# A deeper ring of early weight loads, and the context loaded behind the modulation weights

## The chip, the cores and the metric

One core of a Trainium2 chip runs the whole program. The metric is the time of one execution in microseconds, as the device measures it. The kernel before was run three times: 2746.86 us in the median, from 2741.91 to 2751.96.

## What is computed

Sequence x has 512 tokens, a context 256 tokens, the model width is 2048. Both are normalised, scaled and shifted by a modulation that is worked out from a conditioning vector, and projected to the queries, keys, values and gates of four kinds of attention (branches A to D). The attention outputs go through a gated output projection and are added to x. Two further layers of the same sort follow. The part at the start, which the change touches, reads in short:

```python
mod = silu(c) @ w_ada + b_ada            # shift, scale, gate: 3 x 2048
h   = rms_norm(x,   norm_g) * (1 + scale_x) + shift_x
hc  = rms_norm(ctx, norm_g) * (1 + scale_c) + shift_c
y   = h  @ w_in                          # all projections of the sequence
yc  = hc @ w_in[:, context columns]      # keys and values of the context
...
x   = x + gate * (attention(y, yc) @ w_out)
```

Every product is in float32. The kernel splits each operand into a rounded part (fp32r) and the remainder, and forms three products of 128x512 from the two pairs.

## The kernel before

**Order.** The program's steps are Python generators. At build time a list scheduler runs them against its own table of costs and a clock, and fixes one order of instructions for each engine: PE (TensorE), ACT (ScalarE), DVE (VectorE), POOL (GpSimd) and SP (SyncE, which issues the loads). A step asks for a slot of a pool of buffers, waits for an event, or names an engine and a cost. Each engine runs its row of instructions in order; a change of a slot or a mark therefore moves rows on every engine.

**Weight stream.** `stream()` (L499) takes the list of weight units, each 128x512 float32 (256 KB), two of them a pair. `loads()` issues the pairs on SP, each into the slots that `ring(i)` (L515) names: a pair takes one slot of `wr`, one of `pt`, or two of `P`, in turn, for the first 160 units. There are two slots of 1024 columns in `wr` and in `pt`, five of 768 in `P` and three of 768 in `p`; `pt`, `P` and `p` are pools of the attention and stand empty at the start. `hi()` writes the rounded half of a unit on ACT (L554), `lo()` the remainder on POOL or DVE (L564), and `main()` runs the products in the order of the units. A slot comes free when both units of its pair have been used. After issuing pair i//2, `loads()` sets a mark of that number; other loads wait for marks.

**First units.** There are 128 modulation units (`ada_units`, L630): shift and scale, four blocks each of 512 columns. Their weights go to TensorE as they are, in groups of four units (L667). When a block is whole, `finish()` copies the sums, transposes them by a product with `sel` (L641) and writes `modv` (L647, L656). Among them stand 24 units of six projections: a quarter of the depth (512 of the 2048 rows) of each of six tiles, in four rounds. The shift and scale of quarter b allow the hx blocks of that quarter, and the six units of quarter b follow in the stream. The six of the last quarter end it. The text calls the stretches with the products of these rounds the first to the last quarter. Their accumulators are two tiles named px, one pc, two S and one O. After them come the tiles of keys and values, which take x and the context together.

**Inputs.** `inputs()` (L705) loads x and the context four blocks of 128 rows at a time (`xt`, L717), each load behind a mark; `XMARK` and `CMARK` give the first mark and the distance. It squares every block on ACT (L729), adds on DVE or POOL (L734, L744), and forms the reciprocal norm (L391, L358 to L365, L376, L380, L383). `make_h()` (L758) makes the blocks hx of x and hc of the context from it: a product with the norm (L772, DVE or POOL), scale and shift on ACT (L786), and the split into two parts (L288 on ACT, L291 on DVE or POOL). In the kernel before the context's marks are 40, 46, 52 and 58.

**Behind it.** `gate()` (L673) loads the 64 blocks of gate weights (`gw`, L269) and sums them on DVE (L693, L695); it starts when the last hc block is made. `tables()` builds the tables of relative positions with L1646.

Of the kernel before, what the change touches and what calls it, by code (L numbers as in the profile page):

```python
# [16 lines left out]
DRAM = bass.MemoryType.DRAM  # L17

KT = 16
EARLY = 160  # L20
LAG = (12, 4)
WAYS = 3
EARLY_OUT = ["px", "px", "pc"]
D_ORDER = "r0 q0 h0 q1 g0 h1 g1 r1 g2 q2 h2 g3 q3 - h3"
XMARK = (4, 0.4)
CMARK = (40, 6)
EPS = 1e-6
NEG = -1e30
LOG2 = math.log(2)
# [12 lines left out]
def f32(ap):  # L42
    return ap.bitcast(F32)
# [136 lines left out]
def D(n=0, x2=False, k=1, ptr=0):  # L180
    return ("DVE", k * (0.075 + n * (0.52e-3 if x2 else 1.04e-3) + 0.053 * ptr))
# [7 lines left out]
def A(n=0, ptr=0, acc=0, k=1):  # L189
    return ("ACT", k * (0.1 + n * 0.833e-3 + 0.093 * (ptr + acc)))  # L190


def G(n=0, k=1, bias=0.0):

    return ("POOL", k * (0.1 + n * 2.2e-3), bias)
# [13 lines left out]
class Net:  # L209
# [294 lines left out]
    def stream(self):  # L504

        ready = [Ev() for _ in self.units]
        raws = [Ev() for _ in range((len(self.units) + 1) // 2)]
        left = [min(2, len(self.units) - i) for i in range(0, len(self.units), 2)]
        nc = self.nc

        def whole(i):

            return len(self.units[i]) > 2

        def ring(i):  # L515

            return (["wr"], ["pt"], ["P", "P"], ["wr"], ["pt"], ["P", "P"])[i // 2 % 6] if i < EARLY else ["wr"]

        def wring(i):
            return ("w", "act")[i % 2] if i < EARLY else "w"  # L520

        def loads():
            for i in range(0, len(self.units), 2):
                n = min(2, len(self.units) - i)
                tags = ring(i)
                raw = yield from self.alloc(tags[0], name="wr")
                raw = [raw[:, :512], raw[:, 512:]] if len(tags) == 1 else [raw[:, :512]]
                if len(tags) > 1:
                    raw.append((yield from self.alloc(tags[1], name="wr"))[:, :512])
                src = [self.units[i + j][0] for j in range(n)]  # L530
                if n == 2 and len(tags) == 1 and src[1].offset == src[0].offset + 512:
                    both = bass.AP(tensor=raw[0].tensor, offset=raw[0].offset, ap=[raw[0].ap[0], [1, 1024]])
                    x = src[0]
                    src = [bass.AP(tensor=x.tensor, offset=x.offset, ap=[x.ap[0], [1, 1024]])]
                    dst = [both]
                else:
                    dst = raw
                for x, y in zip(dst, src):
                    yield ("SP", 0.06)
                    nc.sync.dma_start(x, y)  # L540
                self.dma_free = max(self.dma_free, self.s.now) + 1.46
                self.s.set_at(raws[i // 2], self.dma_free + 1.9, raw)
                self.s.set(self.marks.setdefault(i // 2, Ev()))

        def hi():
            for i in range(len(self.units)):
                yield raws[i // 2]
                r = raws[i // 2].val[i % 2]
                if whole(i):
                    self.s.set(ready[i], r)  # L550
                    continue
                w = yield from self.alloc(wring(i), (2, 512), F32R, "w")
                yield A(512)
                nc.scalar.activation(w[:, 0], r, AF.Copy)  # L554
                self.spawn(lo(i, w, r), 1)

        def used(i):
            left[i // 2] -= 1
            if left[i // 2] == 0:
                self.free(*ring(i))  # L560

        def lo(i, w, r):
            e = yield [D(512), G(512, bias=WSLACK)]
            (nc.gpsimd if e == "POOL" else nc.vector).tensor_tensor(w[:, 1], r, f32(w[:, 0]), op=OP.subtract)  # L564
            used(i)
            self.s.set(ready[i], w)

        def main():
            for i, (_, fn, *_) in enumerate(self.units):
                if fn is None:  # L570
                    continue
                if whole(i):
                    for j in range(i, i + 4):
                        yield ready[j]
                    yield from fn([ready[j].val for j in range(i, i + 4)])
                    for j in range(i, i + 4):
                        used(j)
                    continue
                yield ready[i]
                w = ready[i].val  # L580
                yield from fn(w[:, 0], w[:, 1])
                self.free(wring(i))
        self.spawn(loads(), 0)
        self.spawn(hi(), 1)
        self.spawn(main(), 9)
# [633 lines left out]
    def block1(self):  # L1219
# [55 lines left out]
        def ctx():  # L1275
            rc = (yield from self.alloc("b", name="rc"))[:, :256]
            cs, cfin = self.inputs(a["cT"], 256, rc, 4, *CMARK)
            self.make_h(cs, cfin, 256, rc, 1, mods, hc, 4)
# [1098 lines left out]
```

## Time and profile before

| what | value |
|---|---|
| median of three runs | 2746.86 us (2741.91 to 2751.96) |
| profiled execution, its own time | 2743.26 us |
| its span in the profile | 2741.2 us |
| TensorE busy | 2659.6 us, 97% of the span |
| VectorE, ScalarE, GpSimd busy | 1471.3, 1164.1, 1098.7 us |
| DMA | 315.98 MB, 115 GB/s in the mean |
| instructions | 36539 |

The span is the stretch that the profile shows; the execution's own time lies 2.1 us above it. Busy times add up what each engine did. TensorE's products are pipelined, so one row of 0.39 us stands in a dense row of products every 0.23 us. "PEclk" is the clock that was granted to TensorE as a share of its full speed. A note in brackets after an instruction of a timeline gives the idle time before it and what ended that.

### The profile page before, as it was taken

How to read it: one execution, taken by the hardware profiler on the slowest of the kernel's cores; microseconds unless marked ns; L12 is line 12 of the kernel's file. 1: busy time of each engine (PE TensorE's matmuls, PEld its weight loads, DVE VectorE, ACT ScalarE, POOL GpSimd, SP SyncE). 2: the span in 40 equal slices, each digit the busy share in tenths (PEclk: the TensorE clock that was granted, in tenths of full speed). 3: DMA queues.
4: the chain of work that ended last, by engine and by line, in shares of the span. 5: the costliest groups of instructions: out<-in, count | busy, mean ns of one | idle time of the engine just before them, and what ended most of it. 6: DMA issues, size and time to landing. Idle time of an engine off the chain costs nothing.

```text
span 2741.2 us, 36539 instructions
## 1 busy us (share of the span) xinstructions
PE 2659.6 (97%) x13324; PEld 2189.9 (80%) x13324; DVE 1471.3 (54%) x3242; ACT 1164.1 (42%) x2361; POOL 1098.7 (40%) x886
## 2 busy tenths in 40 slices
PE   7889999999999999999999999999999999999999
PEld 3468888888888887788888878777888888888887
DVE  2457753336552656522368576765215877777500
ACT  3444433333332455433442445454334555555421
POOL 1351333334333333344445544445444333344544
PEclk8989999999999999999999999999999999999999
DMA  9845542222221213244222322224442222222443
GB/s 348 301 166 182 171 144 75 76 72 74 70 71 61 70 65 112 88 144 144 85 85 93 108 85 87 90 78 142 148 140 91 94 87 99 90 80 85 143 139 126
DMA packets 121960, 315.98 MB, mean 115 GB/s; under 512 B 13874, under 2 KB 23986, under 8 KB 121780
## 3 DMA queue, kind: packets, MB, share of 16 engines
q1 hardware_dynamic: 121780, 313.65, 34.4%
q8 instruction: 104, 1.70, 0.3%
q14 instruction: 76, 0.62, 0.1%
HBM read 293.02 MB, written 32.11 MB: 119 GB/s over the span
## 4 chain that ended last, share of the span: by engine, by line
PE 80%; DVE 13%; DMA 2%; ACT 2%; issue 1%; POOL 1%; SPq 0%; DVEq 0%; POOLq 0%; ACTq 0%
PE px L491 20%; PE px L492 20%; PE px L493 20%; PE T L398 4%; PE S L1113 2%; PE pc L496 1%; PE pc L498 1%; PE pc L497 1%; DVE P L1803 1%; DVE P L1815 1%; PE T L412 1%; DVE P L314 1%; PE O L1088 1%; PE O L1089 1%; DVE sm L1820 1%
## 5 line engine op out<-in xcount | busy, mean ns | idle before, releaser
L564 POOL TENSOR_TENSOR w<-wr,w 128x512 fp32r<-128x512 f32 x696 | 919.5, 1322 | 1423.1 <-ACT w L554 1419.0
L554 ACT ACTIVATE w<-wr 128x512 fp32r<-128x512 f32 x736 | 463.2, 630 | 948.4 <-PE px L493 616.0
L491 PE MATMUL px<-u,w 128*128 128x512 f32 x1248 | 498.5, 399 | 0.0
L492 PE MATMUL px<-u,w 128*128 128x512 f32 x1248 | 488.8, 392 | 0.0
L493 PE MATMUL px<-u,w 128*128 128x512 f32 x1248 | 488.4, 391 | 0.0
L491 PE MATMUL px<-hx,w 128*128 128x512 f32 x816 | 331.9, 407 | 9.4 <-ACT w L554 6.3
L492 PE MATMUL px<-hx,w 128*128 128x512 f32 x816 | 323.2, 396 | 2.2 <-POOL hx L291 2.2
L493 PE MATMUL px<-hx,w 128*128 128x512 f32 x816 | 322.3, 395 | 1.7 <-POOL w L564 1.7
L491 PE MATMUL px<-o,w 128*128 128x512 f32 x752 | 295.0, 392 | 3.3 <-ACT o L288 3.3
L492 PE MATMUL px<-o,w 128*128 128x512 f32 x752 | 294.3, 391 | 0.5 <-DVE o L291 0.5
L493 PE MATMUL px<-o,w 128*128 128x512 f32 x752 | 294.0, 391 | 0.0
L493 PEld LDWEIGHTS px<-u,w 128*128 128x128 f32 x1248 | 234.8, 188 | 51.3
L491 PEld LDWEIGHTS px<-u,w 128*128 128x128 f32 x1248 | 236.1, 189 | 40.7 <-issue 0.3
L492 PEld LDWEIGHTS px<-u,w 128*128 128x128 f32 x1248 | 235.7, 189 | 39.6
L291 DVE TENSOR_TENSOR pt<-T,pt 128x512 fp32r<-128x512 f32 (+2 forms) x208 | 127.0, 616 | 111.7 <-ACT pt L288 110.3
L493 PEld LDWEIGHTS px<-hx,w 128*128 128x128 f32 x816 | 154.9, 190 | 38.7 <-POOL w L564 3.3
L491 PEld LDWEIGHTS px<-hx,w 128*128 128x128 f32 x816 | 155.7, 191 | 32.9 <-ACT w L554 9.0
L492 PEld LDWEIGHTS px<-hx,w 128*128 128x128 f32 x816 | 155.7, 191 | 19.8 <-POOL hx L291 2.7
L491 PEld LDWEIGHTS px<-o,w 128*128 128x128 f32 x752 | 142.2, 189 | 33.4 <-ACT o L288 4.0
L492 PEld LDWEIGHTS px<-o,w 128*128 128x128 f32 x752 | 142.1, 189 | 30.5 <-DVE o L291 1.1
L493 PEld LDWEIGHTS px<-o,w 128*128 128x128 f32 x752 | 142.0, 189 | 29.3
L1598 DVE TENSOR_TENSOR xr<-px,xr 128x512 f32<-128x512 f32 x32 | 22.1, 692 | 251.0 <-PE px L493 248.1
(343 smaller groups left out, 4365.2 us busy)
## 6 DMA issues: line engine op xcount, KB each, us to landing
wr<-w SPq DMA_DIRECT2D x237, 512.0 KB, 3.5
wr<-wout SPq DMA_DIRECT2D x89, 512.0 KB, 4.2
wr<-wada SPq DMA_DIRECT2D x37, 512.0 KB, 6.8
gw<-wada SPq DMA_DIRECT2D x64, 256.0 KB, 5.3
wr<-w SPq DMA_DIRECT2D x58, 256.0 KB, 4.0
wr<-wada SPq DMA_DIRECT2D x54, 256.0 KB, 6.0
x<-xr SPq DMA_DIRECT2D x32, 256.0 KB, 4.3
xr<-x SPq DMA_DIRECT2D x32, 256.0 KB, 4.5
```

Source lines behind the costliest of these rows:

```text
L291: eng.tensor_tensor(lo, src, f32(hi), op=OP.subtract)
L314: self.nc.vector.tensor_scalar(dst, src, col, None, op0=OP.mult)
L398: self.nc.tensor.transpose(p[:, j * 128:(j + 1) * 128], x, self.ident)
L412: nc.tensor.matmul(p[:, j * gq:(j + 1) * gq], sq[:, j * 128:(j + 1) * 128], self.ones[:, 0:1] if gq == 1 else self.halves, start=True, sto ...
L491: mm(px, hi[:, s], x[0], **kw)
L492: mm(px, hi[:, s], x[1], start=False, stop=False)
L493: mm(px, lo[:, s], x[0], **ke)
L496: mm(pc, lo[:, s], c[0], **kw)
L497: mm(pc, hi[:, s], c[0], start=False, stop=False)
L554: nc.scalar.activation(w[:, 0], r, AF.Copy)
L564: (nc.gpsimd if e == "POOL" else nc.vector).tensor_tensor(w[:, 1], r, f32(w[:, 0]), op=OP.subtract)
L1113: self.nc.tensor.matmul(o, l, r, start=i == 0, stop=i == len(ops) - 1)
```

## The change

The ring of the early units takes turns over seven pairs instead of three: the two slots of one more pair come from the pool `p`, and the turn is wr, pt, P P, p p, wr, pt, P P, so that 14 units instead of 12 can be ahead, up to unit 140. From there to unit 160 the old turn holds. The context's marks become 66, 69, 72 and 75. Lines after L517 of the changed file are numbered two higher.

```diff
-EARLY = 160
+EARLY = 140, 160
...
-CMARK = (40, 6)
+CMARK = (66, 3)
...
         def ring(i):
 
-            return (["wr"], ["pt"], ["P", "P"], ["wr"], ["pt"], ["P", "P"])[i // 2 % 6] if i < EARLY else ["wr"]
+            if i < EARLY[0]:
+                return (["wr"], ["pt"], ["P", "P"], ["p", "p"], ["wr"], ["pt"], ["P", "P"])[i // 2 % 7]
+            return (["wr"], ["pt"], ["P", "P"])[i // 2 % 3] if i < EARLY[1] else ["wr"]
 
         def wring(i):
-            return ("w", "act")[i % 2] if i < EARLY else "w"
+            return ("w", "act")[i % 2] if i < EARLY[1] else "w"
```

TensorE's rows are the same in number and kind, and the orders of all engines differ only in about the first 300 us. Three places follow.

ACT at the start of the third quarter, before; `b` are blocks being made, `hx` the rounded half of a block, L729 squares of the context, and L554 the rounded half of the first weights of the quarter:

```order
L786 ACTIVATE b_825<-b_825,modv 128x512
L288 ACTIVATE hx_835<-b_825 128x512
L786 ACTIVATE b_826<-b_826,modv 128x512
L288 ACTIVATE hx_837<-b_826 128x512
L786 ACTIVATE b_827<-b_827,modv 128x512
L288 ACTIVATE hx_839<-b_827 128x512
L786 ACTIVATE b_828<-b_828,modv 128x512
L288 ACTIVATE hx_853<-b_828 128x512
L729 ACTIVATE b_802<-xt_790 128x256
L729 ACTIVATE b_804<-xt_790 128x256
L729 ACTIVATE b_816<-xt_790 128x256
L554 ACTIVATE w_847<-wr_833 128x512
```

The same place of the changed kernel:

```order
L788 ACTIVATE b_795<-b_795,modv 128x512
L288 ACTIVATE hx_805<-b_795 128x512
L788 ACTIVATE b_796<-b_796,modv 128x512
L288 ACTIVATE hx_807<-b_796 128x512
L556 ACTIVATE w_776<-wr_773 128x512
L788 ACTIVATE b_797<-b_797,modv 128x512
L288 ACTIVATE hx_809<-b_797 128x512
L788 ACTIVATE b_798<-b_798,modv 128x512
L288 ACTIVATE hx_822<-b_798 128x512
L556 ACTIVATE w_848<-wr_817 128x512
```

The squares of the context are gone from here, and the half of the weights (L556 now) stands behind two hx blocks instead of four.

SP where the context's last two loads stood before (`xt<-cT`):

```order
L540 DMA wr_730<-w 128x512
L540 DMA wr_733<-wada 128x1024
L717 DMA xt_728<-cT 128x1024
L540 DMA wr_755<-wada 128x1024
L540 DMA wr_757<-wada 128x512
L540 DMA wr_758<-wada 128x512
L540 DMA wr_780<-wada 128x1024
L540 DMA wr_786<-wada 128x1024
L540 DMA wr_791<-wada 128x512
L540 DMA wr_792<-wada 128x512
L717 DMA xt_790<-cT 128x1024
```

SP where they stand in the changed kernel, `wada` being modulation weights and `w` the weights of projections:

```order
L542 DMA wr_937<-wada 128x512
L542 DMA wr_954<-wada 128x512
L542 DMA wr_960<-wada 128x512
L542 DMA wr_960<-w 128x512
L719 DMA xt_963<-cT 128x1024
L542 DMA wr_985<-w 128x512 x2
L542 DMA wr_995<-w 128x512
L542 DMA wr_996<-w 128x512
L542 DMA wr_999<-w 128x512 x2
L719 DMA xt_1003<-cT 128x1024
L542 DMA wr_1034<-w 128x1024
```

Both have moved behind the last modulation weights, among the loads of the last quarter's weights.

DVE at the start of the last quarter, before; `rx` and `rc` are the norms of x and of the context, `modv` the scale and shift:

```order
L305 COPY b_1125<-T_988 128x512
L564 TENSOR_TENSOR w_1129<-wr_1087,w_1129 128x512
L564 TENSOR_TENSOR w_1153<-wr_1095,w_1153 128x512
L647 TENSOR_SCALAR modv<-T_1137,vec 128x2 x4
L772 TENSOR_TENSOR b_1172<-xt_148,rx 128x512
L772 TENSOR_TENSOR b_1173<-xt_148,rx 128x512
L772 TENSOR_TENSOR b_1174<-xt_150,rx 128x512
L772 TENSOR_TENSOR b_1175<-xt_150,rx 128x512
L772 TENSOR_TENSOR b_1179<-xt_790,rc_92 128x256
L291 TENSOR_TENSOR hx_1186<-b_1173,hx_1186 128x512
L291 TENSOR_TENSOR hx_1190<-b_1174,hx_1190 128x512
L291 TENSOR_TENSOR hx_1195<-b_1175,hx_1195 128x512
```

And in the changed kernel:

```order
L305 COPY b_1033<-T_909 128x512
L736 TENSOR_TENSOR b_846<-b_846,b_1028 128x256
L566 TENSOR_TENSOR w_1038<-wr_995,w_1038 128x512
L649 TENSOR_SCALAR modv<-T_1047,vec 128x2 x4
L566 TENSOR_TENSOR w_1073<-wr_999,w_1073 128x512
L774 TENSOR_TENSOR b_1084<-xt_132,rx 128x512
L774 TENSOR_TENSOR b_1085<-xt_132,rx 128x512
L774 TENSOR_TENSOR b_1086<-xt_134,rx 128x512
L774 TENSOR_TENSOR b_1087<-xt_134,rx 128x512
L291 TENSOR_TENSOR hx_1094<-b_1084,hx_1094 128x512
L291 TENSOR_TENSOR hx_1098<-b_1085,hx_1098 128x512
L291 TENSOR_TENSOR hx_1103<-b_1086,hx_1103 128x512
```

The product of a context block has left the place behind the four of x, and the last sums of the context's squares (L736) and two remainders of weights (L566) stand ahead.

## Rows read from the trace of the kernel before

**Rows 1.** Stretches: length, busy us (PE, PEld, DVE, ACT, POOL), clock, DMA share, GB/s.

```profile
0.00:73.00 73.00, 54.36 (x237) 23.89 (x238) 20.39 (x64) 22.63 (x37) 12.13 (x13) 0.86 0.96 349
73.00:107.00 34.00, 30.12 (x156) 17.53 (x154) 10.13 (x25) 11.83 (x23) 9.66 (x8) 0.95 0.93 323
107.00:149.50 42.50, 37.40 (x172) 20.38 (x170) 23.54 (x56) 26.38 (x54) 24.74 (x23) 0.88 0.76 267
149.50:186.00 36.50, 27.42 (x96) 19.47 (x97) 28.65 (x43) 18.91 (x35) 20.13 (x17) 0.77 0.30 97
186.00:250.00 64.00, 63.74 (x378) 55.48 (x377) 38.95 (x70) 20.05 (x39) 12.53 (x9) 1.00 0.63 205
```

**Rows 2.** TensorE's timeline, second quarter: start us, us, engine, line, operation, tiles, count, [idle].

```profile
73.02 0.95 PE L641 MATMUL T<-sel,b 128*128 128x2 f32 x8
...
83.11 0.80 PE L493 MATMUL px<-hx,w 128*128 128x512 f32 x1 [0.67 <-POOL w L564]
...
86.95 1.07 PE L667 MATMUL T<-wr,cst 128*32 128x512 f32 x8
...
106.84 0.95 PE L641 MATMUL T<-sel,b 128*128 128x2 f32 x8
```

**Rows 3.** ScalarE's timeline, start of the second quarter.

```profile
75.24 0.81 ACT L786 ACTIVATE b<-b,modv 128x512 f32<-128x512 f32 x1 [3.71 <-DVE b L772]
...
77.99 0.80 ACT L786 ACTIVATE b<-b,modv 128x512 f32<-128x512 f32 x1
...
80.73 0.40 ACT L729 ACTIVATE b<-xt 128x256 f32<-128x256 f32 x1
81.03 0.61 ACT L554 ACTIVATE w<-wr 128x512 fp32r<-128x512 f32 x1
```

**Rows 4.** TensorE's timeline, third quarter.

```profile
118.82 0.80 PE L493 MATMUL px<-hx,w 128*128 128x512 f32 x1 [0.40 <-POOL w L564]
...
125.09 1.94 PE L667 MATMUL T<-wr,cst 128*32 128x512 f32 x8
...
147.62 0.95 PE L641 MATMUL T<-sel,b 128*128 128x2 f32 x8
```

**Rows 5.** ScalarE's timeline, start of the third quarter.

```profile
110.14 0.82 ACT L786 ACTIVATE b<-b,modv 128x512 f32<-128x512 f32 x1 [1.94 <-DVE b L772]
...
116.54 0.61 ACT L554 ACTIVATE w<-wr 128x512 fp32r<-128x512 f32 x1
```

**Rows 6.** SyncE's DMA queue, third quarter: start us, us that the issues took.

```profile
115.77 12.10 SPq L540 DMA_DIRECT2D wr<-wada  x3
```

**Rows 7.** Stretches inside the third quarter, columns as in rows 1.

```profile
116.00:128.00 12.00, 9.92 (x29) 5.57 (x30) 6.21 (x16) 3.02 (x8) 4.90 (x4) 0.57 0.42 161
128.00:140.00 12.00, 11.94 (x69) 7.37 (x67) 6.96 (x19) 10.33 (x23) 10.34 (x11) 1.00 0.93 305
140.00:150.00 10.00, 8.65 (x48) 5.32 (x40) 4.71 (x9) 6.11 (x12) 10.00 (x9) 1.00 0.75 248
```

**Rows 8.** TensorE's timeline, last quarter and start of the first context tile.

```profile
155.51 0.79 PE L492 MATMUL px<-hx,w 128*128 128x512 f32 x1 [2.22 <-POOL hx L291]
...
175.28 0.80 PE L491 MATMUL S<-hx,w 128*128 128x512 f32 x1 [2.45 <-ACT th L928]
...
178.33 0.79 PE L491 MATMUL S<-hx,w 128*128 128x512 f32 x1 [1.41 <-DVE th L930]
...
185.27 0.39 PE L491 MATMUL px<-hx,w 128*128 128x512 f32 x1
...
185.95 0.28 PE L496 MATMUL pc<-hc,w 128*128 128x256 f32 x1
```

**Rows 9.** The gate's tile gw: ns min/median/max, first and last start.

```profile
L695 DVE SCALAR_TENSOR_TENSOR gacc<-gw,csil,gacc x60: 732/745/1784, 178.2 to 379.9; 128x512 f32<-128x512 f32 x60
```

**Rows 10.** ScalarE's groups for hc, 100 to 260 us: busy us, mean ns, idle.

```profile
L786 ACT ACTIVATE b<-b,modv 128x256 f32<-128x256 f32 x16 | 9.4, 587 | 0.5 <-DVE b L772 0.5
L288 ACT ACTIVATE hc<-b 128x256 fp32r<-128x256 f32 x16 | 6.6, 415 | 0.4
```

## The prediction

> **What bounds the kernel now.** I read the busy times by stretch first, then TensorE's timeline, then ScalarE's, and the DMA queue's last. The stretches of [rows 1] show where anything can be won: from 186 us on TensorE is busy 63.74 of 64 us at a granted clock of 1.00, while before that it is busy 54.36 of 73, 30.12 of 34, 37.40 of 42.5 and 27.42 of 36.5 us, at 0.86, 0.95, 0.88 and 0.77. Most of what the change moves lies ahead of 186 us. The first 73 us move 349 GB/s at a DMA share of 0.96, so transfers bound them. The third quarter does not look like that: its share is 0.76, and inside it [rows 7] show 161 GB/s at 0.42 between 116 and 128 us, at a clock of 0.57. Here a chain of engines holds the end. TensorE's first remainder product of the quarter runs at 118.82 and waits for GpSimd's remainder of the weights [rows 4]; that waits for ScalarE's rounded half, which starts at 116.54 [rows 5], behind four blocks of hx and squares of the context. Meanwhile three issues of modulation weights take SyncE 12.10 us from 115.77 on [rows 6]: its slots come free only when TensorE has read them. The last quarter starts with a similar chain, and its products wait again at 175.28 and 178.33 [rows 8].
>
> **The change, step by step.** Times are those of the profiled execution: span 2741.2, its own time 2743.26 us. The median of the runs shown is 2746.86, 3.6 us above it; I add 3.6 at the end. The work of every engine stays the same; only the order and the slots of the first 300 us move.
>
> *First quarter, to 73 us.* The ring holds 14 units instead of 12, but bytes at 349 GB/s bound this part [rows 1]: nothing.
>
> *Second quarter.* ScalarE's order puts the rounded half behind two hx blocks instead of four and a square of the context. The blocks start at 75.24 and 77.99 for the first and third, so 1.37 us each; the half started at 81.03 [rows 3]. It can go where the third block stood, at 77.99: 3.0 us earlier. GpSimd's remainder follows it, so the product at 83.11 comes at 80.1, and the modulation group at 86.95 and the sel product at 106.84 [rows 2] come 3.0 us earlier too, since TensorE is dense between them. The two hx blocks that now stand behind the half are needed a few products later; that cover is about 1 us, and if it fails the gain is 2.4. Take −3.0.
>
> *Third quarter.* The context's squares, adds and colsum have left; its loads come behind the modulation weights. ScalarE's first hx block stood at 110.14 [rows 5] and moves to 107.1 with TensorE. The rounded half follows two blocks later, at 109.9, given its weights are there; SyncE issues them earlier because their slot is of a pool that was idle. From half to remainder product took 2.1 us in the second quarter (81.03 to 83.11), so the product comes at 112.0 against 118.82. From there to the first modulation group the second quarter needed 3.84 us (83.11 to 86.95): 115.8 against 125.09. From that group to the sel product it needed 19.9 (86.95 to 106.84) where the third needed 22.5 (125.09 to 147.62) [rows 2, 4]. So sel comes at 135.7 against 147.62: −11.9 in all.
>
> The transfers must allow it. Counted over SyncE's issues, the bytes up to the last modulation weights are 44.11 MB in the new order (45.15 before: two context loads of 524 KB have moved behind). On SyncE these two now stand among the last quarter's own weight loads and hold each of those up by 1.5 us at 349 GB/s, which are wanted after 142 us and have that to spare. 25.5 MB are in by 73 us (73 times 349), so 18.6 MB are wanted by about 131, or 321 GB/s. The second quarter moved 323 [rows 1]. It is enough, with nothing to spare.
>
> *Last quarter's start.* Sel is followed by the row of hx: 2.2 us in the second quarter to the first block (73.02 to 75.24), 1.37 for the block and 0.7 to 0.9 for its remainder, so about 4.5 us: 140.2. Before, it took 7.9 (147.62 to 155.51), because context rows stood among it on VectorE and GpSimd. A new wait stands here instead. ScalarE must first do three squares of the last context load, 0.40 us each [rows 3], and VectorE its adds. The bytes up to that load are 46.99 MB: 21.5 after 73 us, which takes 61.6 us at 349 and 66.6 at 323, so it lands at 134.6 to 139.6. With squares, block and remainder the product comes at 138 to 143.0. Take 141.8, near the late end since 323 is the nearer rate: 155.51 becomes 141.8, −13.7.
>
> *Products of the last quarter.* The waits of 2.45 and 1.41 us at 175.28 and 178.33 [rows 8] are for reads of accumulators by ScalarE and VectorE; in the new order those reads come with all 24 products of S already issued, so −3.9. The mean clock of 0.77 in this stretch [rows 1] cost more: from 155.51 to 185.27 are 29.8 us. A product stretched to full clock takes 0.23 and the 72 of them 16.6, so after the waits 9 us are open to a better clock, less small products. I take 3.0 of those (0 to 6), since a stretch with fewer stops still begins after one. Now −20.6.
>
> *First context tile.* The hc blocks are made late. On ScalarE they cost 0.587 and 0.415 us [rows 10] and now stand behind the q work and amid four weight halves, while TensorE takes one in 0.68 (185.27 to 185.95, [rows 8]) and half as much for three products half as wide, 1.0 us in all. Their makers were off the path before. VectorE's first gate rows (0.745 each, [rows 9]) also stand ahead of a copy that frees an accumulator. Price +1.5, from 0 to 4: none if the first blocks keep their lead, 4 if 8 of them lose 0.5.
>
> **Sum:** −3.0, −8.9 to the sel product, −1.8 to the last quarter, −3.9, −3.0, +1.5: −19.1. 2743.3 becomes 2724.2, and with 3.6 the median **2728**.
>
> **Rivals.** *A, late context loads hold the engines:* if the last load comes at the 305 GB/s of 128 to 140 us [rows 7], it lands at 143.5, and squares, block and remainder give 147 instead of 141.8 (−8.5); with no clock regained the whole is −8.5, −3.9, +1.5: −10.9, **2736**. For it speaks that the queue has nothing to spare, against it that 305 was limited by slots.
>
> *B, transfers bound the front:* then only what left the path counts, 1.05 MB, 3.0 us at 349 GB/s: **2744**. DMA shares of 0.96 and 0.93 in the first two quarters [rows 1] speak for it; 0.42, 0.93 and 0.75 in the third [rows 7] against, since a queue that idles does not hold the end. The Trainium skill, page "SBUF — State Buffer", section "A bandwidth-pool intuition that's wrong (but worth ruling out)", gives about 358 GB/s between HBM and a core and calls HBM "almost always your end-to-end bottleneck". By that rule this rival would hold throughout, the 1.05 MB would be worth 2.9 us by its figure (an estimate), and deeper slots nothing. The trace agrees up to 73 us, not at 116 to 150.
>
> *C, slower, the gate becomes the bound:* 60 VectorE rows of 0.745 us [rows 9] and 64 loads of 256 KB stand behind the context's blocks in order, on VectorE and on SyncE. The first row ran at 178.2, 7 us ahead of the first context tile, the last at 379.9. In the new order the 16 blocks, 1.0 us each, and four halves of 0.6 follow the last squares at about 141, so they end at 160 plus the norm's chain and the q work, as late as before or up to 10 us later, while TensorE is some 20 us earlier: the gate loses 20 to 30 us of lead. If softmax and weight loads behind it then hold TensorE by more than the 19 us won, the kernel is slower, by over 0.3% beyond 27. A loss of 30 gives **2758**. Against it: VectorE is busy 38.95 of 64 us and the DMA share is 0.63 from 186 to 250 [rows 1], so much of that lead is caught up.
>
> *D, the two units do nothing,* and all comes from the moved loads: the same time, so its chance lies within the forecast's.
>
> **Chances.** Forecast 0.62, A 0.18, B 0.13, C 0.05, better than the range 0.02. A measurement can tell about 0.3% from no change, 8.2 us: faster is below 2738.6, slower above 2755.1. Forecast, A and the better case are faster, less 0.03 for their late ends: 0.79. Same: B and those ends, 0.16. Slower: 0.05. The range goes from 2717 (clock 6 instead of 3, product at 138, no context wait, and 2.7 of the 5 us by which the fastest run shown lies below the median) to 2742 (A with the context tile at 4 and a product 3 us later). B and C lie outside, 0.18.
>
> **What would show it.** In the changed profile the product at 118.82 should stand near 112, the 12.10 us of SyncE should be gone, sel should stand near 136, the last quarter's first remainder product near 142 and the first context tile near 165 instead of 185. The stretch from 107 us to that tile should show a DMA share near 0.9 and a clock above 0.88. Wrong would be: a wait for weights by DMA at 108 to 130 us (B), a ScalarE wait for the last context load beyond 143 (A), or waits of TensorE for VectorE or hc beyond 4 us between 165 and 380 us (C).

## The result, and the profile after

The changed kernel takes 2732.01 us in the median of seven runs (2726.09 to 2737.89), the kernel before 2746.12 in seven runs of the same time (2741.91 to 2751.96). The ratio is 0.9949, with a 95% interval of 0.9931 to 0.9967: 14 us faster, between 9 and 19. The forecast was 2728 with a range of 2717 to 2742. The profiled execution has a span of 2725.0 us against 2741.2, 16.2 less.

The stretches of the changed kernel, cut at the sel products that end the first, second and third quarter and at the first product with hc, columns as in [rows 1]:

```profile
0.00:70.77 70.77, 50.10 (x238) 22.79 (x239) 20.29 (x64) 23.22 (x38) 10.41 (x12) 0.90 0.98 364
70.77:100.42 29.65, 27.86 (x154) 16.15 (x152) 6.32 (x19) 10.33 (x16) 8.96 (x7) 1.00 0.96 343
100.42:131.39 30.97, 29.18 (x153) 17.46 (x152) 10.59 (x30) 15.31 (x30) 9.31 (x8) 0.94 0.95 340
131.39:165.93 34.54, 26.28 (x111) 20.93 (x110) 31.45 (x54) 18.39 (x35) 18.23 (x15) 0.80 0.26 97
```

The second quarter runs at full clock (0.95 in [rows 1]), the third moves 340 GB/s at a DMA share of 0.95 (267 and 0.76 before), so the queue no longer idles there. The last stretch still has TensorE busy 26.28 of 34.54 us, at a clock of 0.80.

TensorE's timeline of the changed kernel at the places of [rows 2], [rows 4] and [rows 8]; lines behind L517 are two higher:

```profile
70.77 0.95 PE L643 MATMUL T<-sel,b 128*128 128x2 f32 x8
...
77.76 0.50 PE L493 MATMUL px<-hx,w 128*128 128x512 f32 x1 [0.62 <-POOL w L566]
...
100.42 0.95 PE L643 MATMUL T<-sel,b 128*128 128x2 f32 x8
...
107.42 0.54 PE L493 MATMUL px<-hx,w 128*128 128x512 f32 x1 [0.63 <-POOL w L566]
...
111.49 1.07 PE L669 MATMUL T<-wr,cst 128*32 128x512 f32 x8
...
131.39 0.95 PE L643 MATMUL T<-sel,b 128*128 128x2 f32 x8
...
140.58 0.79 PE L492 MATMUL px<-hx,w 128*128 128x512 f32 x1 [1.16 <-DVE hx L291]
...
154.96 0.68 PE L380 MATMUL T<-b,ones 128*128 128x128 f32 x4 [1.63 <-DVE b L376]
...
165.25 0.39 PE L491 MATMUL px<-hx,w 128*128 128x512 f32 x1
...
172.37 0.39 PE L498 MATMUL pc<-hc,w 128*128 128x256 f32 x1 [0.80 <-DVE hc L291]
...
182.83 1.04 PE L1648 MATMUL T<-b,b 33*32 33x512 f32 x2
```

The product that stood at 83.11 stands at 77.76, that of the third quarter at 107.42 instead of 118.82, sel at 131.39 instead of 147.62, and the first context tile at 165.25 instead of 185.27, 20.0 us earlier. The waits for reads of S are gone; in their place TensorE waits 1.63 us for the context's norm (L380) and 0.80 for a block of hc. Two pairs of table products (L1648, L1646 before) have moved behind the tile's start.

SyncE's issue of modulation weights in the third quarter, where three took 12.10 us in [rows 6], and the first of the gate's rows in the form of [rows 9]:

```profile
113.50 1.33 SPq L542 DMA_DIRECT2D wr<-wada  x3
```

```profile
L697 DVE SCALAR_TENSOR_TENSOR gacc<-gw,csil,gacc x60: 730/748/1865, 183.9 to 391.1; 128x512 f32<-128x512 f32 x60
```

The start of the last quarter on VectorE, on GpSimd and on ScalarE. It is the place that went worst. The columns are as in [rows 3]:

```profile
134.19 1.74 DVE L566 TENSOR_TENSOR w<-wr,w 128x512 fp32r<-128x512 f32 x1 [0.64 <-ACT w L556]
135.85 4.07 DVE L774 TENSOR_TENSOR b<-xt,rx 128x512 f32<-128x512 f32 x4
...
135.35 3.42 POOL L736 TENSOR_TENSOR b<-b,b 128x256 f32<-128x256 f32 x3
...
132.98 1.18 ACT L556 ACTIVATE w<-wr 128x512 fp32r<-128x512 f32 x2 [0.52 <-DMA wr<-w]
134.86 1.03 ACT L731 ACTIVATE b<-xt 128x256 f32<-128x256 f32 x3 [0.71 <-DMA xt<-cT]
137.09 0.81 ACT L788 ACTIVATE b<-b,modv 128x512 f32<-128x512 f32 x1 [1.21 <-DVE b L774]
```

From sel to the first product that needs a remainder of hx it takes 9.2 us (131.39 to 140.58), where the forecast had 6.1 and the kernel before took 7.9. VectorE makes a weight remainder at 134.19; its rounded half is the second of the two from 132.98, which had waited 0.52 us for a load. Then come four products of hx in 4.07 us, beside three adds on GpSimd.

### The profile page after: what moved, and what is told of

It is laid out like the page before. It is cut to its first block, busy times and chain, and to the rows that moved or that the text cites. A ratio compares the mean times of both kernels' runs of the same rounds, so it can differ in the third digit from the quotient of the medians.

```text
span 2725.0 us, 36534 instructions
## 1 busy us (share of the span) xinstructions
PE 2647.3 (97%) x13324; PEld 2187.7 (80%) x13324; DVE 1468.9 (54%) x3246; ACT 1165.6 (43%) x2364; POOL 1092.9 (40%) x879
## 4 chain that ended last, share of the span: by engine, by line
PE 80%; DVE 14%; DMA 2%; issue 2%; ACT 1%; POOL 1%; SPq 0%; POOLq 0%; ACTq 0%; DVEq 0%
PE px L491 20%; PE px L492 20%; PE px L493 20%; PE T L398 4%; PE S L1115 2%; PE pc L496 1%; PE pc L498 1%; PE pc L497 1%; DVE P L1805 1%; DVE P L1817 1%; PE T L412 1%; DVE sm L1822 1%; PE O L1090 1%; PE O L1091 1%; DVE sco L2035 1%
## 5 line engine op out<-in xcount | busy, mean ns | idle before, releaser
L566 POOL TENSOR_TENSOR w<-wr,w 128x512 fp32r<-128x512 f32 x696 | 918.7, 1320 | 1429.2 <-ACT w L556 1415.6
L556 ACT ACTIVATE w<-wr 128x512 fp32r<-128x512 f32 x736 | 463.4, 630 | 937.0 <-PE px L493 623.2
L291 DVE TENSOR_TENSOR pt<-T,pt 128x512 fp32r<-128x512 f32 (+2 forms) x208 | 127.0, 615 | 105.2 <-ACT pt L288 103.9
L288 ACT ACTIVATE pt<-T 128x512 fp32r<-128x512 f32 (+2 forms) x208 | 109.7, 534 | 119.4 <-PE O L1091 72.5
```

Source lines behind the costliest of these rows:

```text
L288: nc.scalar.activation(hi, src, AF.Copy)
L291: eng.tensor_tensor(lo, src, f32(hi), op=OP.subtract)
```

## The experiments

Theory 1 was that each part of the change carries a share: the ring the weights of the third quarter, the marks the context's work, and that the end of the last quarter's waits for reads of S is a side effect of the new order. Rival D had the marks carry all, and a further rival, R, the ring.

**e1, the ring alone.**

```diff
-CMARK = (66, 3)
+CMARK = (40, 6)
```

> The ring of 14 units with the context's marks as before (40, 46, 52, 58). Theory 1 (each part carries a share): the deeper ring brings the first quarter's sel product from 73.02 to about 70.8, as in the changed kernel, since it is the ring that raised the first 73 us from 349 to 365 GB/s; the context's squares, adds and load stay in the third quarter, so the remainder product there stays 5 us or more behind the changed kernel's 107.4, and the first context tile starts at 176 to 183 instead of 165.3; time 2 to 8 us under before. Rival D (the ring does nothing): sel at 73.0, first context tile at 185, time that of before within 2 us. Rival R (the ring carries all): first context tile by 168, time 12 to 16 us under before.

Ratio 0.9970 (0.9961 to 0.9980), 8.2 us under before. TensorE, sel of the third quarter, the second wait for S and the first context tile:

```profile
137.37 1.05 PE L643 MATMUL T<-sel,b 128*128 128x2 f32 x8 [0.39 <-DVE b L305]
...
169.22 0.80 PE L491 MATMUL S<-hx,w 128*128 128x512 f32 x1 [2.11 <-DVE th L932]
...
177.37 0.39 PE L491 MATMUL px<-hx,w 128*128 128x512 f32 x1
```

The ring has a share, and not where it was first looked for: sel of the first quarter stands at 73.64, no earlier than before. From there to the third quarter's sel it takes 63.7 us (74.6 before, 60.6 in the changed kernel), though the context's work still stands in that quarter. But the last quarter takes 40.0 us to the tile, where the changed kernel takes 33.9 and the kernel before 37.7.

**e2, the marks alone.**

```diff
-EARLY = 140, 160
+EARLY = 0, 160
```

> The old ring of 12 units with the context's marks at 66, 69, 72, 75. Theory 1: sel of the first quarter stays at 73.0, the second quarter gains its 3 us from ScalarE's order, the third the context's work; the weights of the third quarter come a little later than with the deeper ring, so the sel product of the third quarter stands at 134 to 138 (changed kernel 131.4, before 147.6) and the first context tile at 168 to 172; time 7 to 13 us under before. Rival D (marks carry all): sel of the third quarter at 131 to 133, first context tile by 166.5, time as that of the changed kernel within 2 us. Rival R (the ring carries all): sel of the third quarter beyond 144, time within 3 us of before.

Ratio 0.9984 (0.9975 to 0.9992), 4.1 us under before. TensorE's waits in the last quarter and its tile:

```profile
165.05 1.19 PE L380 MATMUL T<-b,ones 128*128 128x128 f32 x4 [3.88 <-DVE b L376]
...
173.27 0.80 PE L491 MATMUL S<-hx,w 128*128 128x512 f32 x1 [0.85 <-DVE th L932]
...
178.81 0.40 PE L491 MATMUL px<-hx,w 128*128 128x512 f32 x1
```

The first sel is at 74.82, the third quarter's at 137.49: 62.7 us. So either part by itself brings most of what can be had up to there, 11 and 12 of 14 us. They stand in for one another. What they do only together lies in the last quarter: it takes 41.3 us to the tile here. Rivals D and R both fall: 4.1 and 8.2 against 12 together.

**e3, the changed kernel again.**

> The changed kernel once more, beside the others. Every theory: first context tile at 165 to 166 us, time 10 to 18 us under before, so that the parts can be compared on one chip.

Ratio 0.9956 (0.9943 to 0.9968), median 2732.13; tile at 165.8. It repeats.

**e4, the context still later.**

```diff
-CMARK = (66, 3)
+CMARK = (72, 1)
```

> The changed kernel with the context's marks at 72, 73, 74, 75, so that only one of its loads stands ahead of the last quarter's weights and its squares and adds leave the start of the last quarter. Theory 1: in the changed kernel the sel product at 131.4 reached the first remainder product only at 140.6, 9.2 us later, because VectorE's products of hx stood behind a weight remainder and ran beside three adds of squares on GpSimd (4.07 us for four); without these the distance falls to 5.5 to 7 us and the product stands at 137 to 138.5. The context's blocks come later, by 4 to 8 us, so the first context tiles wait for hc by 3 to 7 us in all: time from 1 us less to 4 us more than the changed kernel. Rival (the blocks have lead enough): no wait for hc beyond 1 us, and 2 to 4 us less than the changed kernel. Rival (the load itself was late, not VectorE): the distance stays at 8 to 9 us, since the transfers ahead end no earlier.

Ratio 0.9978 (0.9969 to 0.9987): it loses half of the gain. Its waits, TensorE from 135 to 320 us (sum, times, longest):

```profile
PE px L492 <- DVE hx L291: 3.6, 1, 3.6
PE T L391 <- DVE b L746: 2.5, 1, 2.5
PE pc L496 <- ACT hc L288: 2.3, 1, 2.3
...
PE T L391 <- DVE gacc L697: 2.0, 1, 2.0
```

The distance from sel, which theory 1 expected to fall to 5.5 to 7 us, stays at 8.7. VectorE's four products of hx start sooner, 1.5 us after sel, but take 6.55 us:

```profile
134.18 6.55 DVE L774 TENSOR_TENSOR b<-xt,rx 128x512 f32<-128x512 f32 x4
```

Beside them GpSimd makes six weight remainders (8.81 us from 131.37); e8 shows the same. The waits for hc (2.3) and for the gate's sum (2.0) are those that the slower rival had named: with the context late enough they appear.

**e5, the kernel before with one read moved.** The question was then what the last quarter gains when both parts are there. In the changed kernel the silu of S comes after all 24 products of S, in e1 and e2 between the two halves.

```diff
         first = []
+        second = Ev()
+
+        def late(i, px, free):
+            if i == 4:
+                self.s.set(second)
+            else:
+                yield second
+            yield from self.silu(px, free, th[i - 2])
...
+            elif i in (3, 4):
+                d = lambda px, pc, i=i, free=free: late(i, px, free)
```

> The kernel before, with one edit: the silu of the first half of S waits until the second half's products are issued. It takes the last quarter's two waits on reads of S (2.45 and 1.41 us at 175.28 and 178.33) away and nothing else. Theory 1: both waits are gone, with them some of the low clock, and the first context tile starts 4 to 8 us earlier, at 178 to 182 instead of 185.3; time 3 to 8 us under before. Rival (the reads' place is taken by the next wait, for pc, O or the q work): the tile starts at 184 or later, time within 2 us of before.

Ratio 0.9979 (0.9970 to 0.9988), 6 us under before, without ring or marks. TensorE, sel and tile:

```profile
146.46 0.95 PE L641 MATMUL T<-sel,b 128*128 128x2 f32 x8
...
178.37 0.39 PE L491 MATMUL px<-hx,w 128*128 128x512 f32 x1
```

From sel to tile 31.9 us against 37.7. Both waits are gone and a wait of 1.31 us for a table's load has come.

**e6 and e7, the same edit on either part.**

> The context's marks at 66 to 75 with the old ring, and the silu of S late as in the run before it. With the marks alone the first context tile stood at 179.5 after waits of 0.69 and 0.85 us on S at a low clock, and 3.88 us on the context's norm. Theory 1 (the ring's part of the last quarter is only that the norm and the reads fall behind the S products): the tile comes at 172 to 176, time 6 to 11 us under before. Rival (the wait on the norm carries the rest): the tile stays at 177 or later, time within 2 us of the marks alone (4 us under before).

> The ring of 14 units with the context's marks as before, and the silu of S late. The ring alone had its first context tile at 178.0 with waits of 1.07 and 2.11 us on S. Theory 1: tile at 171 to 175, and since the context's blocks are made early here, nothing is lost behind it; time 11 to 16 us under before, that is as good as the changed kernel (12 to 14 under). Rival: tile at 177 or later, time within 2 us of the ring alone (8 us under before).

e6: ratio 0.9976 (0.9965 to 0.9987), 6.6 us under before, tile at 173.2; the wait on the norm is still there with 3.38 us. e7: 0.9954 (0.9939 to 0.9969), 12.8 us under before. Its sel and tile on TensorE:

```profile
133.84 1.05 PE L643 MATMUL T<-sel,b 128*128 128x2 f32 x8 [0.39 <-DVE b L305]
...
167.51 0.63 PE L491 MATMUL px<-hx,w 128*128 128x512 f32 x1
```

The ring with the late silu is as fast as the changed kernel, with the context's loads where they were. With both at hand the moved loads give nothing that can be measured. Beside e5, which has neither part, the ring adds 6.7 us and the marks in e6 add 0.6, which can't be told from nothing. The tile of e7 starts 2.3 us later than the changed kernel's, but by 398 us it is 17.1 us ahead of before, and the changed kernel at the same product 17.6: in e7 the context's blocks are early and the tables stay where they were.

The moved loads give part of their gain back behind the tile. Counted from the first quarter's sel in each profile, the changed kernel, e3, e2 and e6 lose 2.6 to 3.9 us of their lead over before between the first product with hc and a wait of 2.13 us that all kernels have (at 902 us before). e4 loses 9.9 there. e1, e5, e7 and e10, with the marks of before, lose less than 0.1.

**e8, the last weights' remainders on GpSimd.**

```diff
-            e = yield [D(512), G(512, bias=WSLACK)]
+            e = yield G(512) if 146 <= i < 152 else [D(512), G(512, bias=WSLACK)]
```

> The changed kernel with the remainders of the last quarter's six weights all on GpSimd, so that VectorE's four products of hx stand right behind the modulation vector, and three adds of squares move from GpSimd to VectorE behind them. Theory 1 (the two weight remainders and the adds beside them held VectorE): the distance from the sel product (131.4 to 132.6) to the first product that needs a remainder of hx falls from 9 us to 5.5 to 7.5, the first context tile stands at 162 to 164.5 instead of 165.3 to 166, and the time is 1 to 4 us below the changed kernel. Rival (the last context load holds ScalarE): the distance stays above 8.5 and the time is that of the changed kernel.

Ratio 0.9956 (0.9943 to 0.9968), that of the changed kernel. VectorE, GpSimd and TensorE:

```profile
133.65 6.01 DVE L774 TENSOR_TENSOR b<-xt,rx 128x512 f32<-128x512 f32 x4
...
130.13 7.32 POOL L566 TENSOR_TENSOR w<-wr,w 128x512 fp32r<-128x512 f32 x5 [0.91 <-PE T L669]
...
141.40 0.80 PE L492 MATMUL px<-hx,w 128*128 128x512 f32 x1 [3.74 <-DVE hx L291]
```

VectorE was free at 133.65, 1.5 us after sel instead of 4.5, and then took 6.01 us for four products, so that the distance stays at 9.2. Neither theory had that: the two engines hold one another up.

**e9 and e10, VectorE alone.** In both the remainders of the last six weights and the products of the last four hx blocks and of hc are forced onto VectorE, with the silu late; e9 from the changed kernel with the context's adds on VectorE too, e10 from the ring alone.

```diff
-            e = yield [D(512), G(512, bias=WSLACK)]
+            e = yield D(512) if 146 <= i < 152 else [D(512), G(512, bias=WSLACK)]
...
-            e = yield [D(n), G(n)]
+            e = yield D(n) if k >= 12 or n == 256 else [D(n), G(n)]
```

> The changed kernel with the work around the last quarter's start taken off GpSimd: the six weight remainders, the context's adds and the products of the last four hx blocks and of the context all on VectorE, the silu of S late. In the run before, VectorE's four products of hx took 6.01 us beside GpSimd's remainders (1.89 us for three in the second quarter with GpSimd idle). Theory 1 (the two engines slow one another): the four take 2.5 to 3.2 us, the distance from the sel product to the first product that needs a remainder of hx falls from 9.2 to 6 to 7.5 us, the first context tile comes at 162 to 164, the time is 1 to 4 us below the changed kernel. Rival (the last context load holds them, since VectorE's add of its square stands ahead): the products start no earlier than 136 and the distance stays above 8, time that of the changed kernel.

> The ring of 14 units, the context's marks as before, the silu of S late (12.8 us under before in the run of that kernel), and in the last quarter the weight remainders and the products of hx and hc on VectorE alone. Theory 1: the distance from the sel product to the first product that needs a remainder of hx falls from 7.6 to 5.5 to 7 us and the later stop of 0.84 us goes; first context tile at 165.5 to 168 against 168.8, time 13 to 17 us under before. Rival (VectorE's longer row of products for hc then stands ahead of the copies of the q work): distance shorter, but the tile at 168.5 or later and the time that of the ring with the late silu.

e9: ratio 0.9993 (0.9983 to 1.0003), the gain is lost. VectorE's four products, and TensorE's wait in the tile:

```profile
135.97 2.49 DVE L774 TENSOR_TENSOR b<-xt,rx 128x512 f32<-128x512 f32 x4
...
172.84 1.87 PE L412 MATMUL T<-ones,b 128*128 128x1 f32 x8 [10.92 <-ACT b L408]
```

The four take 2.49 us with GpSimd idle, so the slowing is shown. But they start at 135.97, behind six remainders and an add, and the distance is 8.5 us. What TensorE waits for at the end of it is GpSimd, in the split of hx (L291), which the edit left free to either engine:

```profile
140.99 0.80 PE L492 MATMUL px<-hx,w 128*128 128x512 f32 x1 [2.14 <-POOL hx L291]
138.25 4.11 POOL L291 TENSOR_TENSOR hx<-b,hx 128x512 fp32r<-128x512 f32 x2 [8.77 <-ACT hx L288]
```

So e9 doesn't show how short the distance can get. The wait of 10.92 us is this edit's own: all sixteen products of hc stand on VectorE ahead of a copy of px, at 168.04, that the q work needs. e10: 0.9943 (0.9931 to 0.9955), 15.2 us under before, tile at 165.23; the distance is 9.9 us, again behind a split on GpSimd (1.97), so the gain is not for the reason expected. It has the lowest ratio of all, though its interval overlaps that of the changed kernel, so that I call it as good, not better.

## Why the prediction was right

The sign, the place and the range were right. By the steps, in the profiled executions:

| step | forecast | measured |
|---|---|---|
| first quarter, to sel | 0 | −2.25 |
| second quarter, sel to sel | −3.0 | −4.2 |
| third quarter, sel to sel | −8.9 | −9.8 |
| sel to first remainder product | −1.8 | +1.3 |
| from there to the first context tile | −6.9 | −5.1 |
| first context tile and behind | +1.5 | +3.8 |
| span | −19.1 | −16.2 |

The size came out smaller: 14 us in the medians, where 19 were forecast, and 14.0 in the profiles too, once the −2.25 of the first quarter is left out. Two of the signs it named did not come. From 107 us to the first context tile the DMA share is 0.56 and the clock 0.85, where it had near 0.9 and above 0.88; by its own sum the last of these loads land by 140 us, so the share could not stand near 0.9 to 165.

*First quarter.* The −2.25 is not shown to be part of the change. The sel product that ends it stands at 70.8 to 73.8 in kernels with the ring of 14 units (after, e1, e3, e4, e7 to e10) and at 71.5 to 74.8 in those without (before, e2, e5, e6). Transfers bound it, and what they give differs from one execution to the next: the changed kernel and e4 have the same order up to 108 us, and their sel stands at 70.77 and 73.80, after 366 and 352 GB/s in the first 70 us. My expectation for e1 had taken it for the ring's work.

*Second and third quarter.* Right in size. That the half of the weights stands behind two hx blocks was the reason in the second: the first remainder product comes 7.0 us after sel instead of 10.1. The other 1.1 us come behind it, where the products of before started 0.43 us apart and now start 0.23 apart. The third's remainder product came at 107.4 instead of 112.0, in part through the earlier start. But the forecast put the third quarter's gain down to both parts, as if each had its piece. The runs e1 and e2 show that either is enough for most of it.

*Start of the last quarter.* The step "about 4.5 us after sel, or the last context load" failed in its price. ScalarE's three squares at 134.86 did wait for that load, as the step and rival A said; but what came last was VectorE, behind a weight remainder and slowed by GpSimd's adds. Undisturbed rows of the second quarter (three products in 1.89 us) had been taken for a place where both engines work. The quantity that was right for it stood in the trace before: 7.9 us in the same place, with these rows:

```profile
149.70 4.63 DVE L772 TENSOR_TENSOR b<-xt,rx 128x512 f32<-128x512 f32 x4
150.35 3.43 POOL L772 TENSOR_TENSOR b<-xt,rc 128x256 f32<-128x256 f32 x3
```

The prediction had put the 7.9 down to these context rows and took them to be gone; in the changed kernel three adds of the context's squares stand in their place. So the slowing was there before, 4.63 us against 4.07, and what the change added is the late start of the four, 4.5 us after sel instead of 2.1.

*Products of the last quarter.* The two waits went, −3.9, and e5 shows that this alone is worth 6 us of the time. The rest of the −5.1 adds up as: +1.6 for the wait on the norm, which was not foreseen; +0.8 for the context's products with ones and for its norm, which moved in (0.36 and 0.44 from start to start); −1.9 for two pairs of table products, which moved out; which leaves −1.7, put down to the clock, where the forecast had −3.0.

*Behind the tile.* The table products that moved out come back, 1.9 us, and the hc block costs 0.8. By 902 us of before the changed kernel is 17.4 us ahead. The last 1.2 go where both kernels have the same order. The changed kernel behind a wait that both have:

```profile
884.75 0.44 PE L398 MATMUL T<-ident,p 128*128 128x128 f32 x2 [2.13 <-DVE p L448]
...
885.84 0.65 PE L491 MATMUL px<-hx,w 128*128 128x512 f32 x1
886.28 0.63 PE L492 MATMUL px<-hx,w 128*128 128x512 f32 x1
```

and the kernel before:

```profile
902.14 0.44 PE L398 MATMUL T<-ident,p 128*128 128x128 f32 x2 [2.13 <-DVE p L448]
...
903.23 0.48 PE L491 MATMUL px<-hx,w 128*128 128x512 f32 x1
903.54 0.39 PE L492 MATMUL px<-hx,w 128*128 128x512 f32 x1
903.77 0.40 PE L493 MATMUL px<-hx,w 128*128 128x512 f32 x1
```

After the same wait of 2.13 us the products stand 0.44 us apart in one and 0.31, then 0.23, in the other: a stretch at the low clock (0.52 from 885.84 to 889.27, against 1.00 from 903.23 to 905.40), 0.2 us for each product. e1 to e8 and e10 show such a stretch there too, among them e5, whose order on TensorE is that of before; the profiles of before and of e9 do not. Since the order is the same I don't count it to the change.

*The rivals.* B is refuted: e1 takes no transfer off the path and e5 none, and they gain 8.2 and 6 us. The rule of the Trainium skill that stood beside it, in "SBUF — State Buffer", section "A bandwidth-pool intuition that's wrong (but worth ruling out)", fits the third quarter only now, when it moves 340 GB/s; it was a chain of engines that kept the queue below that, since e2, with the old ring, moves 347 GB/s there too. A was right that late loads stand ahead of the last quarter, and wrong on when: ScalarE's squares of the last one start at 134.86, not behind 143.5, and the gain is 14, not 11. C named the right waits: the gate's last row starts at 391.1 instead of 379.9, but with the change no wait for it is longer than 0.2 us; in e4 it is 2.0. D is refuted by e2.

What stays open is why ring and marks together lead the planner to put the reads of S late, and either alone does not. e5 to e7 show what it is worth, not how the order came about.

## What to carry to other kernels

When a scheduler fixes the orders, a moved load changes rows far from it: test each part alone, and look for the wait whose loss the parts share. Here one read moved by hand behind the products of its accumulator gave 6 us without the change, and with the ring alone as much as the whole change. Price a chain by rows from a place where the same engines are busy at once, not by the cleanest rows of the trace.

## What the runs showed of the hardware

VectorE's product of two operands, 128x512, took 0.62 us each with GpSimd idle (2.49 for four, e9), and GpSimd's weight remainder 1.28 by itself:

```profile
106.08 1.28 POOL L566 TENSOR_TENSOR w<-wr,w 128x512 fp32r<-128x512 f32 x1 [8.46 <-ACT w L556]
```

Side by side, in e8, the two engines go in step:

```profile
135.74 1.71 POOL L566 TENSOR_TENSOR w<-wr,w 128x512 fp32r<-128x512 f32 x1
137.41 1.71 POOL L566 TENSOR_TENSOR w<-wr,w 128x512 fp32r<-128x512 f32 x1
136.24 1.75 DVE L774 TENSOR_TENSOR b<-xt,rx 128x512 f32<-128x512 f32 x1
137.92 1.75 DVE L774 TENSOR_TENSOR b<-xt,rx 128x512 f32<-128x512 f32 x1
```

From one start to the next it is 1.67 us on GpSimd and 1.68 on VectorE: one remainder and one product in that time. Beside GpSimd's adds of 128x256, in the changed kernel, the step is 1.13 us on both (VectorE 136.98 to 138.11, GpSimd 136.47 to 137.60). The 1.5 us that follow from 6.01 for four are a mean, since the first of them took 0.99.

The Trainium skill, "SBUF — State Buffer", section "Who interferes with whom", says that a VectorE instruction with two inputs in SBUF contends with a GpSimd instruction that reads SBUF for a shared port pair, which one holds for its whole instruction while the other is blocked. The runs agree that the two take turns. Blocked for the whole of each instruction, a pair would take 0.62 and 1.28, 1.9 us; the measured 1.68 is 0.2 less.
